# Modulation sums along rows, operand tiles placed 128 bytes in or out of step, a fifth slot in the weight ring, and the linear attention's operands written in place

## The chip, the cores and the metric

The kernel runs on one core of a Trainium2 chip. The metric is the device time of one execution in microseconds. Before the change it is 2567.68 us, the median of 3 timed runs (2567.05 to 2570.22). A profile was taken of one further execution.

## The reference

All tensors are float32. There are 256 tokens of width 2048. The first block has two layers of `x = x + concat(conv, differential attention, memory attention) @ w_out`, all fed from one product `rmsnorm(x) @ w_in`. The second block is a token mixer and a feed-forward network, both modulated by a vector that is worked out from `c`:

```
c_act = silu(c)
mod = c_act @ w_mod + b_mod                     # 2048 -> 6 * 2048
sh1, sc1, g1, sh2, sc2, g2 = split(mod, 6)
h = rms_norm(x, mix_norm_pre) * (1 + sc1) + sh1
y = token_mixer(h, ...)                         # window attention + gated linear attention
x = x + g1 * rms_norm(y, mix_norm_post)
h = rms_norm(x, ffn_norm_pre) * (1 + sc2) + sh2
y = conv_ffn(h, w_up, conv_w, conv_b, w_down)
x = x + g2 * rms_norm(y, ffn_norm_post)
```

In the gated linear attention, `q_in = q * exp(b)` and `k_st = k * exp(b_last - b)` are made for each head, besides `q * exp(b - b_mid)` and `k * exp(b_mid - b)`. In the FFN, `u = h @ w_up` goes through a causal convolution of width 3, and `(silu(gate) * val) @ w_down` gives y, with 5632 gate and 5632 value columns.

## The kernel before

**Precision.** Every large product is made of three. An operand is split into a high part (rounded to the type fp32r) and the low part that is left over, and hi x hi, hi x lo and lo x hi are added up in PSUM; "a triple" is these three matmuls. `gemm_as` (lines 354 to 356) holds x stationary and streams the weight, 512 columns wide. `gemm_ws` (lines 406 to 408) holds the weight stationary and streams x, 256 tokens wide. `gemm_wsu` (lines 428 to 430) is like `gemm_ws` with 258 columns. The split tiles of x are pairs: C and D (hi and lo), or A and B.

**The weight ring.** All weights come as pieces of 512 KB, 128 partitions x 1024 elements, in one list. `load` (line 222) issues a piece's DMA on SP's queue into one of four slots (`RB`, tile `raw`). `consume` splits a weight piece: ACT copies raw to `hi`, DVE writes `lo` = raw - hi, each with four buffers (`HB`). Right behind that in the program stands the load of the piece four places further on, which has to wait until the slot's readers are done. 847 pieces are weights of products, and 192 are of `w_mod`.

**The order.** The program is written out in its final order; nothing reorders it on an engine. Beside the pieces run small generators (attention, norms, convolution, evacuations), which `tick` moves on after every item. `await_tasks(name)` runs ticks until a generator has set the flag of that name. `spread_mod` puts the 192 modulation pieces between the weight pieces: 64 in the layers, 96 in the mixer, 32 in the FFN, and in stretches marked heavy at 0.45 of the density.

**The modulation.** A piece of `w_mod` holds 2 x 128 rows (k, on partitions) of 512 columns. DVE multiplies each row block with its 128 values of silu(c) (`ca`, one per partition) and adds it to `macc` [128 x 512]: two instructions a piece, and eight pieces to a block of 512 columns. Then `mod_done` adds up over the partitions: DVE makes two transposes within 32 x 32 blocks and two reductions into `mred`, and after four such blocks PE multiplies `mred` with a matrix of ones (into a bank `pb`), and four DVE additions write the result plus `b_mod` to `modT`, which holds one column of 128 values per block.

**Where the tiles lie.** A, B, C, D and the buffers of hi and lo are of 16 KB per partition or smaller multiples of 256 bytes. C and D (`hT`, the normalised x of the mixer and the FFN) follow each other 16,384 bytes apart. A is 128 bytes longer, since in other places it holds the 258-wide tiles, so B begins 16,512 bytes behind A. `pair_AB` gives A and a view of B that is shifted by 32 elements (128 bytes), so that it begins a multiple of 256 bytes behind A; the mixer uses it for the linear attention's output `obT`. The FFN's `gv`, the operand of `w_down`, are A and B as they are. Here "in step" is a pair whose distance is a multiple of 256 bytes, and "out of step" one that is 128 bytes off.

**The products.** The layers' `w_in` streams A and B through `gemm_ws`, out of step. The mixer's three merging products and its `w_out` (1400 to 1720 us) use `gemm_as`. The FFN's `w_up` has 176 pieces, 16 of them through `gemm_wsu` and 160 through `gemm_ws` with C and D, 8 triples each; its `w_down` has 88 pieces of 4 triples through `gemm_as` and its variant for halves (lines 379 to 381), with A and B.

Except for matmuls, most instructions are recorded by one helper, so they have line 133 in the profile (145 after the change, as 12 lines are added above it). Its tiles are told by name: `tm`, `t1k`, `e2k` are scratch, `ml` and `mh` the merged operand.

Of the kernel before, what the change touches and what calls it, by code (L numbers as in the profile page):

```python
# [6 lines left out]
F32 = mybir.dt.float32  # L7
F32R = mybir.dt.float32r
# [3 lines left out]
ALU = mybir.AluOpType  # L12
AX = mybir.AxisListType

P = 128
D = 2048
# [5 lines left out]
C_ID, C_ONE, C_INV, C_SWA, C_SCAN, C_GLA, C_SUM, C_DIST, C_END = 0, 128, 256, 288, 672, 928, 1056, 1184, 1696  # L22
# [4 lines left out]
R_BMOD, R_CW2, R_CB2 = 256, 352, 616  # L27
# [33 lines left out]
    return [512] * (n // 512)  # L61


def row_tiles(n):

    return 16 if n == 16 else 1024 // n


def lay_pieces(np, name, w):

    layers, rows, n = w.shape
    out, c0 = np.empty((layers, rows * n), w.dtype), 0
    for width in cuts(name, n):
        src = w[:, :, c0:c0 + width].reshape(layers, -1, row_tiles(width), P, width).transpose(0, 1, 3, 2, 4)
        out[:, rows * c0:rows * (c0 + width)].reshape(src.shape)[:] = src
        c0 += width
    assert c0 == n
    return out
# [75 lines left out]


class Kernel:
    RB = 4
    HB = 4
    NBG = 3
    CAP = 4.5  # L160
# [302 lines left out]
    def setup(self, ctx):  # L463
        nc, tc, a = self.nc, self.tc, self.a
        pool = lambda name, **k: ctx.enter_context(tc.tile_pool(name=name, bufs=1, **k))
        self.cp = pool("consts")
        self.wp = pool("weights")
        self.ap = pool("acts")
        dp = pool("dram", space=bass.MemoryType.DRAM)
        self.scr = {n: dp.tile(s, F32, tag=n, name=n) for n, s in (  # L470
            ("x1", [2 * P, D]), ("x2", [2 * P, D]), ("x3", [2 * P, D]), ("gp1", [D]), ("gp2", [D]))}
        self.psA = ctx.enter_context(tc.tile_pool(name="psA", bufs=2, space=bass.MemoryType.PSUM))
        psB = pool("psB", space=bass.MemoryType.PSUM)
        self.ps = Slots(psB, "pb", 4, 512)
        self.tm = Slots(self.ap, "tm", 4, 1024)
        self.sm = Slots(self.cp, "sm", 14, 16)
        self.t1 = Slots(self.ap, "t1k", 2, 256)

        cst = self.cp.tile([P, C_DIST], F32, tag="cst", name="cst")
        self.cst = cst  # L480
        self.ident = cst[:, C_ID:C_ID + P]
        self.ones = cst[:, C_ONE:C_ONE + P]
        self.junk = self.cp.tile([P, 512], mybir.dt.bfloat16, tag="junk", name="junk")
        self.mhalf = self.cp.tile([P, 16], F32, tag="mhalf", name="mhalf")
        self.cols = self.cp.tile([P, 704], F32, tag="cols", name="cols")
        self.modT = self.cp.tile([P, 96], F32, tag="modT", name="modT")
        raw = self.st["xraw"] = self.ap.tile([P, 16, 256], F32, tag="X16", name="xraw")
        for k in range(2):
            self.x_load(k, 1, nc.act_dma)
        nc.vector.memset(self.mhalf, -0.5)  # L490
        self.sg = self.sm_tile("sg", [P, 6])
        self.ca = self.sm_tile("ca", [P, 16])
        nc.scalar.activation(out=self.ca, in_=self.mhalf, func=AF.Identity)
        self.warm_up()
# [15 lines left out]
    def params(self):  # L510
        nc, a = self.nc, self.a
        nc.sync.dma_start(out=self.cols[:, 64:], in_=a["cols"][:, 64:])
        pos = self.sm_tile("pos_i", [P, 2], I32)
        nc.sync.dma_start(out=pos, in_=a["pos_cols"])
        yield
        for _ in range(6):
            yield
        nc.vector.tensor_copy(self.col(R_POS, 2), pos)


        th = self.sm.get()
        nc.scalar.activation(out=th, in_=self.col(R_C, 16), func=AF.Tanh, scale=0.5)
        nc.vector.scalar_tensor_tensor(out=self.ca, in0=th, scalar=1.0, in1=self.col(R_C, 16), op0=ALU.add, op1=ALU.mult)
        nc.vector.tensor_scalar(out=self.ca, in0=self.ca, scalar1=0.5, scalar2=None, op0=ALU.mult)
        self.sm.put(th)
        yield


        for l in range(2):
            for j, (r, s) in enumerate(((R_DQ, 0.125), (R_MQ, P ** -0.5), (R_HG, 1.0 - self.lam_init(l)))):  # L530
                nc.vector.tensor_scalar(out=self.sg[:, 3 * l + j:3 * l + j + 1], in0=self.col(r + l), scalar1=s,
                                        scalar2=None, op0=ALU.mult)

        yield
        self.st["params"] = True

    def params_attn(self):
        nc, a = self.nc, self.a
# [56 lines left out]

    def plan_mod(self):

        nc = self.nc
        self.mod_queue = deque()
        w = self.weight("w_mod_2")  # L600
        for j in range(24):
            box = {}
            for k0 in range(0, 16, 2):
                def fn(raw, j=j, k0=k0, box=box):
                    if k0 == 0:
                        if j > 1:
                            self.await_tasks(f"red{j - 2}", bg=False)
                        box["acc"] = self.cp.tile([P, 512], F32, tag="macc", name=self.nm("macc"), bufs=2)
                    acc = box["acc"]
                    for kk in range(2):  # L610
                        s = self.ca[:, k0 + kk:k0 + kk + 1]
                        if k0 + kk == 0:
                            nc.vector.tensor_scalar(out=acc, in0=raw[:, kk], scalar1=s, scalar2=None, op0=ALU.mult)
                        else:
                            nc.vector.scalar_tensor_tensor(out=acc, in0=raw[:, kk], scalar=s, in1=acc,
                                                           op0=ALU.mult, op1=ALU.add)
                    if k0 == 14:
                        self.evac.append(self.mod_done(j, acc))
                src = w.piece(k0, 2, j * 512, 512)
                self.mod_queue.append(Item("mod", fn, src, 2, 512))  # L620

    def mod_done(self, j, acc):

        nc = self.nc
        yield
        if j % 4 == 0:
            self.mred = self.cp.tile([P, 64], F32, tag="mred", name=self.nm("mred"), bufs=2)
        red = self.mred
        while not self.t1.ok():
            yield  # L630
        for h in range(2):
            tr = self.t1.get()
            nc.vector.transpose(tr, acc[:, 256 * h:256 * h + 256])
            b = 16 * (j % 4) + 8 * h
            nc.vector.tensor_reduce(out=red[:, b:b + 8], in_=tr.rearrange("p (b i) -> p b i", i=32), axis=AX.X, op=ALU.add)
            self.t1.put(tr)
        self.st[f"red{j}"] = True
        if j % 4 < 3:
            return
        yield  # L640
        yield
        pt = self.bank()
        nc.side.matmul(pt[:, 0:64], self.cst[:, C_SUM:C_SUM + P], red, start=True, stop=True)
        for q in range(4):
            b = slice(32 * q, 32 * q + 32)
            nc.vector.tensor_tensor(out=self.modT[b, 4 * j - 12:4 * j + 4],
                                    in0=pt[b, 0:64].rearrange("p (c q) -> p q c", q=4)[:, q],
                                    in1=self.cols[b, R_BMOD + 4 * j - 12:R_BMOD + 4 * j + 4], op=ALU.add)
        self.ps.put(pt)
        for i in range(4):  # L650
            self.st[f"mod{j - i}"] = True

    def mod_row(self, gcol, postcol, dst):

# [237 lines left out]
    def layer(self, l, last):  # L892
        nc, st, a = self.nc, self.st, self.a
# [136 lines left out]
        def out_begin():  # L1030
# [8 lines left out]
            if last:  # L1039
                self.await_tasks(*[f"mod{j}" for j in range(8)])  # L1040
                self.shifted("G1", R_MIXPRE, 16, 0)
                st["raw"] = [self.lp.tile([P, 4, 256], F32, tag=t, name=self.nm("raw")) for t in ("dv", "dg", "mkT", "mg")]
            else:
                st["xT2"] = [self.ap.tile([P, 16, 256], F32R, tag=t, name=self.nm(t)) for t in ("A", "B")]
# [305 lines left out]
    def shift_norm(self):  # L1350
# [15 lines left out]
        self.t1.put(dg)  # L1366
        self.ps.put(pt)
        st["r_ready"] = True
        hi, lo = [self.ap.tile([P, 16, 256], F32R, tag=t, name=self.nm(t)) for t in ("C", "D")]
        st["hT"] = (hi, lo)  # L1370
        us = [raws[k // 4][:, k % 4:k % 4 + 2] for k in range(0, 16, 2)]
        for i in range(9):
# [238 lines left out]
    def gla_pair(self, c):  # L1611
# [5 lines left out]
        for hh in range(2):  # L1617
# [1 line left out]
            q, k = qb[:, 2 * hh:2 * hh + 2], kb[:, 2 * hh:2 * hh + 2]  # L1619
            Bh = st["b"][:, 2 * h:2 * h + 2]  # L1620
            b8 = v8(Bh)
            Q, K, QI, KS, K2, QD = V(0), V(1), V(2), V(3), V(4, (2, P)), V(5, (2, 64))
            while not self.e2.ok(2):
                yield
            d, e = self.e2.get([P, 2, 256]), self.e2.get([P, 2, 256])
# [331 lines left out]
    def open_f(self):  # L1957
# [4 lines left out]
        self.st["raw"] = [self.fp.tile([P, 4, 256], F32, tag=f"raw{n}", name=self.nm("raw")) for n in range(4)]  # L1962
        self.st["u"] = 0
        self.st["h_ready"] = self.st["r_ready"] = self.st["u_done"] = False

    def add_x(self, n, tb):

# [30 lines left out]
    def ffn(self):  # L1998
# [153 lines left out]
        for part in range(3):  # L2152
            chunks = range(4 * part, min(4 * part + 4, 11))

            def alloc():
                st["gv"] = [self.ap.tile([P, 16, 256], F32R, tag=t, name=self.nm(t)) for t in ("A", "B")]

            self.do(alloc)
            for i in chunks:
# [102 lines left out]
```

## Time and profile before

| | us |
|---|---|
| median of 3 timed runs | 2567.68 (2567.05 to 2570.22) |
| the profiled execution | 2563.99 |
| its span, first to last instruction | 2562.2 |
| DVE: the 847 splits (lo) | 1026.8 |
| DVE: the modulation's STT of 512 elements, 360 at 749 ns | 269.7 |
| DVE: its transposes and reductions, 48 each | 20.9 + 20.2 |
| PE: idle in the whole span | 35.4 |
| DMA: loaded and stored | 576.77 MB, mean 225 GB/s |

Times are of the profiled execution unless the table says otherwise. PE is TensorE, PEld its weight loads (they overlap the matmuls), DVE VectorE, ACT ScalarE, POOL GpSimd, SP SyncE, whose queue issues the loads. A row of a group gives line, engine, operation, output<-input, shapes, the number of them, busy time, the mean of one in ns, and behind the last bar the idle time ahead of them and what ended it. Matmuls are pipelined, so their durations overlap: the pace is the distance between starts. "STT" is SCALAR_TENSOR_TENSOR.

### The profile page before, as it was taken

How to read it: one execution, taken by the hardware profiler on the slowest of the kernel's cores; microseconds unless marked ns; L12 is line 12 of the kernel's file. 1: busy time of each engine (PE TensorE's matmuls, PEld its weight loads, DVE VectorE, ACT ScalarE, POOL GpSimd, SP SyncE). 2: the span in 40 equal slices, each digit the busy share in tenths (PEclk: the TensorE clock that was granted, in tenths of full speed). 3: DMA queues.
4: the chain of work that ended last, by engine and by line, in shares of the span. 5: the costliest groups of instructions: out<-in, count | busy, mean ns of one | idle time of the engine just before them, and what ended most of it. 6: DMA issues, size and time to landing. Idle time of an engine off the chain costs nothing.

```text
span 2562.2 us, 38632 instructions
## 1 busy us (share of the span) xinstructions
PE 2526.8 (99%) x15079; PEld 2227.7 (87%) x15079; DVE 1823.1 (71%) x2469; ACT 1266.9 (49%) x1826; POOL 52.0 (2%) x43
## 2 busy tenths in 40 slices
PE   9999999999999999999999999999999999999998
PEld 7889998788899989878988778777999899988996
DVE  6768767786786756777777777775777667765665
ACT  6645544564554455355454334344744444543443
POOL 1000000010010000000000000000000000000000
PEclk9999999999999999999999999999999999999999
DMA  8775568887656576755558888886566766676655
GB/s 311 225 255 181 179 197 271 299 272 256 220 179 190 180 249 187 224 173 190 193 182 267 285 290 286 280 289 210 164 215 231 230 215 214 223 236 197 198 188 174
DMA packets 168903, 576.77 MB, mean 225 GB/s; under 512 B 18272, under 2 KB 24576, under 8 KB 168720
## 3 DMA queue, kind: packets, MB, share of 16 engines
q1 hardware_dynamic: 168432, 574.04, 69.0%
q8 instruction: 118, 1.93, 0.3%
q14 instruction: 65, 0.53, 0.1%
q10 hardware_dynamic: 288, 0.26, 0.0%
HBM read 565.83 MB, written 8.40 MB: 224 GB/s over the span
## 4 chain that ended last, share of the span: by engine, by line
PE 77%; DMA 9%; DVE 8%; ACT 3%; issue 2%; POOL 0%; ACTq 0%; DVEq 0%; POOLq 0%
PE acc L355 13%; PE acc L356 13%; PE acc L354 13%; PE acc L406 10%; PE acc L407 10%; PE acc L408 10%; PE pb L133 5%; DMA raw<-w_in 4%; DVE lo L133 4%; ACT hi L133 2%; DMA raw<-w_out 2%; DMA raw<-w_branch_gla 1%; DVE macc L133 1%; DMA raw<-w_branch_attn 1%; DVE tm L133 1%
## 5 line engine op out<-in xcount | busy, mean ns | idle before, releaser
L133 DVE TENSOR_TENSOR lo<-raw,hi 128x1024 fp32r<-128x1024 f32 (+1 forms) x847 | 1026.8, 1220 | 515.7 <-ACT hi L133 511.2
L133 ACT CAST hi<-raw 128x1024 fp32r<-128x1024 f32 (+1 forms) x847 | 881.7, 1048 | 867.6 <-PE acc L356 281.4
L408 PE MATMUL acc<-C,lo 128*128 128x256 f32 (+1 forms) x1424 | 403.0, 283 | 0.8 <-DVE lo L133 0.8
L406 PE MATMUL acc<-C,hi 128*128 128x256 f32 (+1 forms) x1424 | 403.7, 284 | 0.0
L407 PE MATMUL acc<-D,hi 128*128 128x256 f32 (+1 forms) x1424 | 402.9, 283 | 0.0
L354 PE MATMUL acc<-hi,C 128*128 128x512 f32 x992 | 393.1, 396 | 0.0
L355 PE MATMUL acc<-lo,C 128*128 128x512 f32 x992 | 387.4, 390 | 4.0 <-DVE lo L133 3.9
L356 PE MATMUL acc<-hi,D 128*128 128x512 f32 x992 | 387.0, 390 | 0.0
L355 PE MATMUL acc<-lo,A 128*128 128x512 f32 x904 | 357.7, 396 | 1.2 <-DVE lo L133 1.1
L356 PE MATMUL acc<-hi,B 128*128 128x512 f32 x904 | 357.9, 396 | 0.0
L354 PE MATMUL acc<-hi,A 128*128 128x512 f32 x904 | 354.2, 392 | 0.7 <-ACT hi L133 0.7
L133 DVE SCALAR_TENSOR_TENSOR macc<-raw,ca,macc 128x512 f32<-128x512 f32 x360 | 269.7, 749 | 9.9 <-DMA raw<-w_mod 2.9
L406 PEld LDWEIGHTS acc<-C,hi 128*128 128x128 f32 (+1 forms) x1424 | 271.7, 191 | 1.5 <-issue 0.7
L408 PEld LDWEIGHTS acc<-C,lo 128*128 128x128 f32 (+1 forms) x1424 | 271.7, 191 | 1.4 <-DVE lo L133 1.0
L407 PEld LDWEIGHTS acc<-D,hi 128*128 128x128 f32 (+1 forms) x1424 | 271.8, 191 | 0.6
L406 PE MATMUL acc<-A,hi 128*128 128x256 f32 x896 | 256.3, 286 | 0.0
L407 PE MATMUL acc<-B,hi 128*128 128x256 f32 x896 | 252.0, 281 | 0.0
L408 PE MATMUL acc<-A,lo 128*128 128x256 f32 x896 | 251.2, 280 | 0.3 <-DVE lo L133 0.2
L355 PEld LDWEIGHTS acc<-lo,C 128*128 128x128 f32 x992 | 186.4, 188 | 45.5 <-DVE lo L133 7.9
L354 PEld LDWEIGHTS acc<-hi,C 128*128 128x128 f32 x992 | 186.3, 188 | 40.5 <-issue 3.4
L356 PEld LDWEIGHTS acc<-hi,D 128*128 128x128 f32 x992 | 186.2, 188 | 39.3
L354 PEld LDWEIGHTS acc<-hi,A 128*128 128x128 f32 x904 | 172.7, 191 | 40.9 <-ACT hi L133 1.6
(269 smaller groups left out, 2989.5 us busy)
## 6 DMA issues: line engine op xcount, KB each, us to landing
raw<-w_in SPq DMA_DIRECT2D x406, 512.0 KB, 4.4
raw<-w_mod SPq DMA_DIRECT2D x192, 512.0 KB, 4.6
raw<-w_up SPq DMA_DIRECT2D x176, 512.0 KB, 4.2
raw<-w_out SPq DMA_DIRECT2D x96, 512.0 KB, 4.5
raw<-w_down SPq DMA_DIRECT2D x88, 512.0 KB, 4.3
raw<-w_mem_kv SPq DMA_DIRECT2D x32, 512.0 KB, 4.4
raw<-w_branch_gla SPq DMA_DIRECT2D x32, 512.0 KB, 4.7
tm<-x SPq DMA_DIRECT2D x20, 512.0 KB, 6.2
```

The source lines that it names most:

```text
L133: return f(*args, **kw)
L354: nc.tensor.matmul(o, xh[:, kt, t], hi, start=s, stop=False)
L355: nc.tensor.matmul(o, xh[:, kt, t], lo, start=False, stop=False)
L356: nc.tensor.matmul(o, xl[:, kt, t], hi, start=False, stop=e)
L406: nc.tensor.matmul(o, hi[:, c], xh, start=s and j % 2 == 0, stop=False, skip_group_check=True)
L407: nc.tensor.matmul(o, hi[:, c], xl, start=False, stop=False, skip_group_check=True)
L408: nc.tensor.matmul(o, lo[:, c], xh, start=False, stop=e, skip_group_check=True)
```

## The change

1. **Modulation.** The host lays `w_mod` out by output columns: a piece is 128 columns (on partitions) by 1024 of the 2048 k. One DVE instruction per piece (`tensor_tensor_reduce`, written in place over raw) multiplies it with `crow`, a tile that holds half of silu(c) on every partition, and sums along the row into one column of `mpart` (first half) or `modT` (second half, begun from `mpart`). The pieces' order is `MOD_GROUPS`: in each of three groups of blocks all first halves, then all second ones. So `crow` is filled six times, once by `c_row` (PE transposes `ca`, DVE copies it out, a DMA writes it to DRAM, another one reads it back to all partitions) and five times by `crow_load`, two ticks after the last sum on the old half. A sum waits for its half. `mod_done`, with its transposes, reductions, matmuls and additions, is gone; one addition of `b_mod` for four blocks takes its place.
2. **Ring.** `RB` is 5 instead of 4.
3. **Linear attention.** QI and KS are written over q and k, and K2 and QD take the tiles V2 and V3. V4 and V5 are gone.
4. **Tiles.** In the FFN, `hT`'s low tile D begins 32 elements (128 bytes) later (`skew`), and `gv` uses `pair_AB`. The mixer's `hT` keeps a skew of 0.

The core of the diff:

```diff
+MOD_GROUPS = ((0, 8), (8, 20), (20, 24))
+def mod_order():
+    return [(h, b) for j0, j1 in MOD_GROUPS for h in range(2) for b in range(4 * j0, 4 * j1)]
...
+    if name == "w_mod_2":
+        half = [w[:, 1024 * h:1024 * h + 1024, P * b:P * b + P].transpose(0, 2, 1) for h, b in mod_order()]
+        return np.stack(half, 1).reshape(layers, rows * n)
...
-    RB = 4
+    RB = 5
...
+        self.mpart = self.cp.tile([P, 96], F32, tag="mpart", name="mpart")
+        self.crow = self.cp.tile([P, 1024], F32, tag="crow", name="crow")
...
-        for j in range(24):
-            box = {}
-            for k0 in range(0, 16, 2):
-                def fn(raw, j=j, k0=k0, box=box):
...
-                            nc.vector.scalar_tensor_tensor(out=acc, in0=raw[:, kk], scalar=s, in1=acc,
-                                                           op0=ALU.mult, op1=ALU.add)
-                    if k0 == 14:
-                        self.evac.append(self.mod_done(j, acc))
+        order = mod_order()
+        for i, (h, b) in enumerate(order):
+            def fn(raw, i=i, h=h, b=b):
+                self.await_tasks(f"crow{self.mod_half[i]}", bg=False)
+                d = raw.rearrange("p k n -> p (k n)")
+                out = self.mpart[:, b:b + 1] if h == 0 else self.modT[:, b:b + 1]
+                nc.vector.tensor_tensor_reduce(out=d, in0=d, in1=self.crow, scale=1.0,
+                                               scalar=0.0 if h == 0 else self.mpart[:, b:b + 1], op0=ALU.mult, op1=ALU.add,
+                                               accum_out=out)
+                if h and b % 4 == 3:
+                    j = b // 4
+                    nc.vector.tensor_tensor(out=self.modT[:, b - 3:b + 1], in0=self.modT[:, b - 3:b + 1],
+                                            in1=self.col(R_BMOD + b - 3, 4), op=ALU.add)
+                    self.st[f"mod{j}"] = True
+                if i + 1 < len(order) and self.mod_half[i + 1] != self.mod_half[i]:
+                    self.evac.append(self.crow_load(self.mod_half[i + 1]))
...
+    def crow_load(self, m):
+        for _ in range(2 if m else 0):
+            yield
+        h = m % 2
+        self.nc.sync.dma_start(out=self.crow, in_=self.scr["crow"][1024 * h:1024 * h + 1024].partition_broadcast(P))
+        self.st[f"crow{m}"] = True
...
-        hi, lo = [self.ap.tile([P, 16, 256], F32R, tag=t, name=self.nm(t)) for t in ("C", "D")]
+        hi = self.ap.tile([P, 16, 256], F32R, tag="C", name=self.nm("C"))
+        lo = self.ap.tile([P, 16 * 256 + 64], F32R, tag="D", name=self.nm("D"))
+        s = st["skew"]
+        lo = lo[:, s:s + 4096].rearrange("p (k t) -> p k t", t=256)
...
-            Q, K, QI, KS, K2, QD = V(0), V(1), V(2), V(3), V(4, (2, P)), V(5, (2, 64))
+            Q, K, QI, KS, K2, QD = V(0), V(1), q, k, V(2, (2, P)), V(3, (2, 64))
...
+        self.st["skew"] = 32
...
-                st["gv"] = [self.ap.tile([P, 16, 256], F32R, tag=t, name=self.nm(t)) for t in ("A", "B")]
+                st["gv"] = self.pair_AB()
```

DVE, at the end of the mixer's modulation, in `w_out` of the mixer: what stood there before (`macc` is the running sum, `mred` its reduction, `pb` a PSUM bank that PE has filled).

```order
L133 SCALAR_TENSOR_TENSOR macc_15328<-raw_15538,ca,macc_15328 128x512 x2
L133 TENSOR_TENSOR lo_15604<-raw_15556,hi_15603 128x1024
L133 TENSOR_TENSOR lo_15628<-raw_15578,hi_15627 128x1024
L133 SCALAR_TENSOR_TENSOR ml<-pb_213_15621,mh 128x512
L133 STREAM_TRANSPOSE t1k_78_15648<-macc_15328 128x256
L133 TENSOR_REDUCE mred_14730<-t1k_78_15648 128x8
L133 STREAM_TRANSPOSE t1k_79_15651<-macc_15328 128x256
L133 TENSOR_REDUCE mred_14730<-t1k_79_15651 128x8
L133 TENSOR_TENSOR lo_15655<-raw_15584,hi_15654 128x1024
L133 TENSOR_TENSOR modT<-pb_214_15672,cols 32x16 x4
```

And the same place on DVE after the change (an ISA row of 128x1024 is the new product with its sum, and the ISA row of 128x1 behind it reads the sum out).

```order
L145 ISA raw_15192,modT<-raw_15192,crow,mpart 128x1024
L145 ISA modT 128x1
L145 TENSOR_TENSOR lo_15285<-raw_15218,hi_15284 128x1024
L145 SCALAR_TENSOR_TENSOR ml<-pb_209_15275,mh 128x512
L145 ISA raw_15237,modT<-raw_15237,crow,mpart 128x1024
L145 ISA modT 128x1
L145 TENSOR_TENSOR modT<-modT,cols 128x4
L145 TENSOR_TENSOR lo_15308<-raw_15243,hi_15307 128x1024
```

The four rows of transposes and reductions between two splits are gone, and so are PE's matmul over `mred` and the four additions that waited for it; a piece has one long and one short row instead of two rows of 512.

SP's queue after the change, where the mixer goes from the window attention's merge (`w_branch_attn`) on to the gate columns of `w_in`, and `crow` is filled for the second half of the second group:

```order
L234 DMA raw_13497<-w_mod 128x1024
L234 DMA raw_13521<-w_branch_attn 128x1024
L234 DMA raw_13537<-w_mod 128x1024
L234 DMA raw_13543<-w_branch_attn 128x1024
L234 DMA raw_13567<-w_branch_attn 128x1024
L234 DMA raw_13583<-w_mod 128x1024
L234 DMA raw_13589<-w_in 128x1024
L646 DMA crow<-crow 128x1024
L234 DMA raw_13605<-w_in 128x1024
```

DVE at that place: the first row is the last sum on the old half, and the fourth, over raw_13537, is the first on the new one.

```order
L145 ISA raw_13497,mpart<-raw_13497,crow 128x1024
L145 ISA mpart 128x1
L145 TENSOR_TENSOR lo_13586<-raw_13521,hi_13585 128x1024
L145 ISA raw_13537,modT<-raw_13537,crow,mpart 128x1024
L145 ISA modT 128x1
L145 TENSOR_TENSOR lo_13608<-raw_13543,hi_13607 128x1024
L145 TENSOR_TENSOR lo_13628<-raw_13567,hi_13627 128x1024
```

Before, nothing of this was on SP's or DVE's queue; the load of `crow` now stands five loads behind that of raw_13537, and one split stands between the last reader of the old `crow` and the first of the new one.

More of the change, by code (lines that the diff above doesn't have):

```diff
@@ L470, in setup @@
         self.scr = {n: dp.tile(s, F32, tag=n, name=n) for n, s in (
-            ("x1", [2 * P, D]), ("x2", [2 * P, D]), ("x3", [2 * P, D]), ("gp1", [D]), ("gp2", [D]))}
+            ("x1", [2 * P, D]), ("x2", [2 * P, D]), ("x3", [2 * P, D]), ("gp1", [D]), ("gp2", [D]), ("crow", [D]))}
         self.psA = ctx.enter_context(tc.tile_pool(name="psA", bufs=2, space=bass.MemoryType.PSUM))
@@ L535, in params @@
         self.st["params"] = True
+        for _ in range(6):
+            yield
+        yield from self.c_row()
     def params_attn(self):
@@ L599, in plan_mod @@
         self.mod_queue = deque()
-        w = self.weight("w_mod_2")
-        for j in range(24):
-            box = {}
-            for k0 in range(0, 16, 2):
-                def fn(raw, j=j, k0=k0, box=box):
[L605 to L614, printed above, removed]
-                            nc.vector.scalar_tensor_tensor(out=acc, in0=raw[:, kk], scalar=s, in1=acc,
-                                                           op0=ALU.mult, op1=ALU.add)
-                    if k0 == 14:
-                        self.evac.append(self.mod_done(j, acc))
-                src = w.piece(k0, 2, j * 512, 512)
-                self.mod_queue.append(Item("mod", fn, src, 2, 512))
@@ L622, in mod_done @@
-    def mod_done(self, j, acc):
-        nc = self.nc
-        yield
[L626 to L639, printed above, removed]
+        order = mod_order()
@@ new lines, in plan_mod @@
+        for i, (h, b) in enumerate(order):
[13 more added lines that the diff above has]
+                    self.evac.append(self.crow_load(self.mod_half[i + 1]))
+            src = self.a["w_mod_2"][0][i * P * 1024:(i + 1) * P * 1024].rearrange("(p k n) -> p k n", p=P, k=2)
+            self.mod_queue.append(Item("mod", fn, src, 2, 512))
@@ new lines, in plan_mod, with c_row @@
+        self.mod_half, m = [], -1
+        for i, (h, b) in enumerate(order):
+            m += i == 0 or h != order[i - 1][0]
+            self.mod_half.append(m)
+    def crow_load(self, m):
+        for _ in range(2 if m else 0):
+            yield
+        h = m % 2
+        self.nc.sync.dma_start(out=self.crow, in_=self.scr["crow"][1024 * h:1024 * h + 1024].partition_broadcast(P))
+        self.st[f"crow{m}"] = True
+    def c_row(self):
+        nc = self.nc
+        pt = self.bank()
+        self.transpose(pt[:16, :P], self.ca)
+        row = self.t1.get([P, 256])
+        nc.vector.tensor_copy(row[:16, :P], pt[:16, :P])
+        self.ps.put(pt)
+        yield
+        nc.sync.dma_start(out=self.scr["crow"].rearrange("(k p) -> k p", p=P), in_=row[:16, :P])
+        self.t1.put(row)
@@ L640, in mod_done @@
         yield
         yield
[L642 to L648, printed above, removed]
@@ L649, in mod_done @@
-        self.ps.put(pt)
-        for i in range(4):
-            self.st[f"mod{j - i}"] = True
+        yield from self.crow_load(0)
     def mod_row(self, gcol, postcol, dst):
@@ L1041, in out_begin @@
                 self.shifted("G1", R_MIXPRE, 16, 0)
+                st["skew"] = 0
                 st["raw"] = [self.lp.tile([P, 4, 256], F32, tag=t, name=self.nm("raw")) for t in ("dv", "dg", "mkT", "mg")]
```

## The prediction

> **What bounds the kernel now.** The head of the profile's page and its chain come first.
>
> ```profile
> span 2562.2 us, 38632 instructions
> PE 2526.8 (99%) x15079; PEld 2227.7 (87%) x15079; DVE 1823.1 (71%) x2469; ACT 1266.9 (49%) x1826; POOL 52.0 (2%) x43
> ...
> PE 77%; DMA 9%; DVE 8%; ACT 3%; issue 2%; POOL 0%; ACTq 0%; DVEq 0%; POOLq 0%
> ```
>
> PE is busy for all but 35 us, so the time falls in two ways only: its matmuls follow each other faster, or it waits less. The chain leaves PE for DMA, DVE and ACT during a fifth of the span. To see where, I read the busy time by stage (PE, PEld, DVE, ACT and POOL, then the granted clock, the DMA share and GB/s).
>
> ```profile
> core 0: us, PE busy (x) PEld busy (x) DVE busy (x) ACT busy (x) POOL busy (x), PEclk, DMA share, GB/s
> 500.00:520.00 20.00, 19.19 (x84) 15.44 (x83) 15.39 (x28) 13.29 (x20) 2.20 (x2) 1.00 0.95 335
> 1400.00:1720.00 320.00, 307.01 (x1336) 246.30 (x1335) 251.38 (x304) 124.93 (x125) 0.00 (x0) 0.99 0.86 288
> 200.00:300.00 100.00, 100.00 (x791) 95.38 (x788) 81.31 (x140) 58.89 (x132) 7.20 (x7) 1.00 0.55 174
> ```
>
> The stretch 1400 to 1720 is the merge of the mixer and its last product. 13.0 of PE's 35 idle us lie there (320.00 less 307.01); 200 to 300 has none. The waits of that stretch, first PE's, then its weight loads', then ACT's (us, times, longest):
>
> ```profile
> PE acc L355 <- DVE lo L133: 5.0, 11, 0.8
> PE pb L133 <- DVE tm L133: 4.2, 3, 2.1
> PE pb L133 <- DVE mred L133: 3.5, 2, 3.3
> ```
> ```profile
> PEld acc L355 <- DVE lo L133: 12.4, 20, 1.1
> PEld pb L133 <- DVE tm L133: 5.7, 4, 2.6
> PEld pb L133 <- DVE mred L133: 4.4, 2, 3.8
> ```
> ```profile
> ACT hi L133 <- DMA raw<-w_in: 83.3, 47, 4.1
> ACT hi L133 <- DMA raw<-w_branch_gla: 44.7, 27, 3.6
> ...
> ACT hi L133 <- PE acc L356: 3.1, 2, 2.7
> ```
>
> PE waits for the split of a piece (lo), and for two small DVE results. DVE is not full (251 of 320). ACT, a step earlier, waits 128 us for landings of two weights and hardly for PE: the pieces come late, not the consumers. The chain from 1410 (start, length) shows why.
>
> ```profile
> 1409.99 5.50 DMA raw<-w_in
> ...
> 1415.60 1.07 ACT hi L133
> ...
> 1416.69 1.24 DVE lo L133
> 1417.94 4.17 DMA raw<-w_branch_gla
> ...
> 1424.55 5.98 DMA raw<-w_branch_gla
> ...
> 1431.72 1.23 DVE lo L133
> ```
>
> Each load starts when the split before it has freed a slot. A slot's turns take 7.95, 6.61 and 8.40 us (1409.99, 1417.94, 1424.55, 1432.95), 7.65 on average: with four slots, one piece every 1.91 us. The stage consumes 110 weight pieces and 62 of modulation (rows below), one every 1.86 us. So this stretch is bound by the **ring of four slots**, and the rest by PE's own pace.
>
> **The change, part by part.**
>
> *Tiles in step.* Four stretches of uninterrupted triples in PE's timeline, first and last row of each (start, length), 11 triples in the first two and 6 in the others:
>
> ```profile
> 854.91 0.28 PE L406 MATMUL acc<-A,hi 128*128 128x256 f32 x1
> ...
> 858.76 0.28 PE L406 MATMUL acc<-A,hi 128*128 128x256 f32 x1
> ```
> ```profile
> 2110.03 0.28 PE L406 MATMUL acc<-C,hi 128*128 128x256 f32 x1
> ...
> 2113.99 0.28 PE L406 MATMUL acc<-C,hi 128*128 128x256 f32 x1
> ```
> ```profile
> 1422.60 0.39 PE L354 MATMUL acc<-hi,A 128*128 128x512 f32 x1
> ...
> 1426.68 0.39 PE L354 MATMUL acc<-hi,A 128*128 128x512 f32 x1
> ```
> ```profile
> 2282.26 0.39 PE L354 MATMUL acc<-hi,A 128*128 128x512 f32 x1
> ...
> 2286.42 0.39 PE L354 MATMUL acc<-hi,A 128*128 128x512 f32 x1
> ```
>
> With the weight stationary, the triple takes 350 ns from A and B (3.85 us over 11) and 360 from C and D (3.96 over 11). With x stationary, it takes 680 ns on the mixer's A and B (4.08 over 6) and 693 on the FFN's (4.16 over 6), with the same names and shapes. What differs is where the low tile begins: 16,384 bytes after the high one (C and D) or 128 more (A and B, whose shifted view in pair_AB brings it back to a multiple of 256). So stationary weights want the pair 128 bytes out of step, and stationary x wants it in step; the change gives the FFN both. The price of the wrong phase is 10 and 13.3 ns a triple. w_up has 176 pieces, 16 of them go through the 258-wide product, and the other 160 have 8 triples: 1280 x 10 = 12.8 us, of which I take **-12**, since busier stretches may hold less. w_down has 88 pieces of 4: 352 x 13.3 = **-4.7**. Both are PE's pace and lie on the path; bounds 0 and -17.5 together. All tiles also begin 96 bytes further on modulo 256; no row here tells what that does, and I take nothing for it.
>
> [...]
>
> *The modulation sums.* DVE's groups in the ring's stretch, and one of the whole run:
>
> ```profile
> L133 DVE TENSOR_TENSOR lo<-raw,hi 128x1024 fp32r<-128x1024 f32 x110 | 134.2, 1224 | 63.3 <-ACT hi L133 62.6
> L133 DVE SCALAR_TENSOR_TENSOR macc<-raw,ca,macc 128x512 f32<-128x512 f32 x117 | 87.7, 749 | 3.4 <-DMA raw<-w_mod 1.1
> ...
> L133 DVE STREAM_TRANSPOSE t1k<-macc 128x256 f32<-128x256 f32 x16 | 7.0, 436 | 0.0
> L133 DVE TENSOR_REDUCE mred<-t1k 128x8 f32<-128x256 f32 x16 | 6.7, 421 | 0.6
> ...
> L133 DVE TENSOR_SCALAR macc<-raw,ca 128x512 f32<-128x512 f32 x7 | 3.4, 480 | 0.0
> L133 DVE TENSOR_TENSOR modT<-pb,cols 32x16 f32<-32x16 f32 x8 | 1.3, 168 | 0.1
> ```
> ```profile
> L133 DVE TENSOR_TENSOR_SCAN b<-cst,gk 128x256 f32<-128x256 f32 x8 | 5.1, 679 | 0.1
> ...
> L133 DVE TENSOR_TENSOR t1k<-acc,cos 128x256 f32<-128x256 f32 x8 | 3.4, 423 | 1.0 <-PE acc L356 0.8
> ```
>
> 117 and 7 halves make 62 pieces. The old sums cost 87.7 + 7.0 + 6.7 + 3.4 + 1.3 = 106.1 us here. The new one is one product with a sum over 1024 elements, which the trace lacks. The nearest row is lo, two f32 sources of the same shape: 1.22 us. From below the 1024 elements could go at TENSOR_SCALAR's 480 ns for 512, 0.96 us; from above stands the scan, whose 256 elements take 256 ns more than a plain product, 1 ns an element, so 1.22 + 1.02 = 2.24 us. I take 1.22, plus 0.17 for the second row that reads the sum out (the 32x16 row). Then 62 x 1.39 + about 8 x 0.17 for the bias adds is 87.6: DVE is 18.5 us less busy there, unseen except through the waits below.
>
> [...]
>
> *The fifth slot.* The same turn of 7.65 us spread over five slots gives a piece every 1.53 us. PE needs 110 pieces x 12 matmuls x 0.227 us (the 680 ns above, by three) = 300 us, 1.74 a piece over 172, so PE becomes the bound again, if the DMA can go at 0.524 MB / 1.74 us = 301 GB/s. It went at 335 for 20 us. What goes of the waits: those for mred altogether, as PE's sums over it no longer exist (3.5 in PE's list, 4.4 in the loads': 3.9); those for lo (5.0 and 12.4, mean 8.7) by four fifths, 7.0; those for tm (4.2 and 5.7), which stand behind splits and modulation sums on DVE, by two fifths, 2.0. Together **-13**; the bounds are 0 and the whole 22.5 of the loads' list. Late next is DVE's own queue.
>
> *The sums' matmuls.* All of PE's, and PE's waits for lo in the whole run:
>
> ```profile
> L133 PE MATMUL pb<-mred,cst x12: 217/273/423, 483.9 to 2324.6; 128*128 128x64 f32 x12
> ```
> ```profile
> PE acc L355 <- DVE lo L133: 6.9, 14, 0.9
> ```
>
> Twelve records at 0.27 us, overlapping by half: **-1.5** (0 to -3.3). Of the lo waits 1.9 lie outside the stage; with a deeper ring most go: **-1.5** (0 to -1.9).
>
> *The row of c.* Five reloads of the tile that every new sum reads. The next sum, and all of DVE behind it, waits for the landing, and so do the splits that PE needs. Each is 512 KB, and starts two ticks after the last sum on the old half. Three of the five have a long time before the next modulation piece. In the order, the mixer's reload stands on SP five loads behind the piece that its user multiplies, and on DVE one split lies between the last sum on the old half and that user: about 1.2 us of cover against 4.2 to 6.0 for a landing (the chain above), so DVE stops for some 4 us. PE then lives on splits made ahead, up to three, each good for 2.7 us (12 x 0.227). I take **+3** (0 to +8), and **+1** (0 to +4) for the one at the layers' boundary. The first c row is made beside the start's other side work, at nothing.
>
> *The rest.* The linear attention's operands written into q and k change no instruction; they could only add a wait where the old tile is still read. For its bound I take one lo row, 1.22 us, in each of the four heads, 4.9 us; PE has other items there and hardly idles outside the ring's stretch, so nothing.
>
> Sum: -12 - 4.7 - 13 - 1.5 - 1.5 + 3 + 1 = -28.7 on the profiled execution's 2564.0 us (its span and 1.8 us around it): 2535.3. That execution lies 3.7 below the median of the runs shown, 2567.7, so the forecast is **2539**.
>
> **The rivals.**
>
> *R1, the tile shifts give nothing*, or the 96 bytes take as much elsewhere. For: no row here has stationary weights on C and D out of step, and the fifth slot moves every tile. Against: the 10 and 13.3 ns come from like shapes at one clock. 2539 + 16.7 = 2556.
>
> *R2, the product with a sum runs at half speed.* At the scan's price DVE has 251.4 - 106.1 + 62 x (2.24 + 0.17) + 1.4 = 296 us of work in the ring's stretch of 320. The densest 100 us that the trace shows are at 0.81; at 0.9 the stretch takes 329, at 0.81 366, in the middle 347, 27 more instead of 13 less. Elsewhere 130 pieces cost 0.7 us more each, mostly hidden: +5. So 2539 + 40 + 5 = 2584, slower than before. It decides from where the stretch takes 320 us at a density of 0.85, 272 us of work: a sum of (272 - 146.7) / 62 = 2.02 us with its read.
>
> *R3, the fifth slot only lengthens the landings*, or the reloads eat it. For: at 0.86 the DMA queues are nearly full, and a transfer that shares them with four others ends later; then the pace stays at 1.86 us. Against: 335 GB/s at 500. Only mred's 3.9 goes, and 2539 + 9 + 4 = 2552.
>
> **How the numbers follow.** Forecast 0.66, with its own range of 2527 to 2553 (the whole of the ring's waits gone and no reload waited for, 12 less; half of the ring's gain and dear reloads, 14 more). R1 0.13, R3 0.13, R2 0.08. The range of 2526 to 2561 holds the forecast and R1 and R3, and leaves out R2 and sums of R1 and R3. A measurement of this kernel tells about 0.2%, 5.1 us, from no change. Faster by more: the forecast, nearly all of R1 and R3, 0.87; within it: both of them together, or a sum at about 2 us, 0.06; slower: most of R2, 0.07.
>
> **What would show it.** The FFN's triples: 350 instead of 360 and 680 instead of 693. The new sum's row: 1.2 to 1.3 us, with a second row below 0.2. Between about 1400 and 1700: no wait for mred, those for lo below 3 us on PE, ACT waiting for PE and not for landings, over 300 GB/s. In the mixer one wait of DVE for the reload, of 3 to 5 us, with PE idle for less. It is wrong if the sum takes over 2 us, if landings grow by as much as the fifth slot gains, or if triples elsewhere (the layers' 350, the mixer's 680) get longer.

## The result and the profile after

The changed kernel takes 2526.97 us (median of 4 runs, 2525.40 to 2527.49) against 2567.36 us for the kernel before in the same session (4 runs, 2564.64 to 2570.22): a ratio of 0.9842, with a 95% interval of 0.9824 to 0.9859, so 40 us or 1.6% faster. The forecast was 2539, 28 us faster. The profiled execution of after took 2527.14 us, 36.85 less than that of before.

The head of the page of after, and its chain:

```profile
span 2525.3 us, 38525 instructions
## 1 busy us (share of the span) xinstructions
PE 2503.0 (99%) x15068; PEld 2217.2 (88%) x15068; DVE 1747.5 (69%) x2374; ACT 1265.4 (50%) x1826; POOL 53.6 (2%) x43
...
PE 95%; DVE 3%; ACT 1%; issue 1%; DMA 0%; SPq 0%; POOL 0%; POOLq 0%; DVEq 0%; ACTq 0%
```

DMA, which was 9% of the chain, is gone from it, and PE went from 77% to 95%. To place the gain, each weight matmul of after was set beside the same one of before (both have 14064 of them in the same order). The difference of their start times is -3.4 us at the matmul that stood at 1400 in the kernel before, -23.9 at 1720, still -23.9 at 1772, and -37.0 at the last one. So 20.4 us come from the mixer's merge and `w_out`, 13.1 from the FFN, and 3.4 from what lies ahead.

The same stretch of work as 1400 to 1720 before now takes 299.4 us, by the starts of its first and last matmul (by stage, columns as before):

```profile
1396.80:1696.70 299.90, 298.83 (x1334) 246.93 (x1333) 225.79 (x273) 124.63 (x124) 0.00 (x0) 1.00 0.88 304
```

PE is full, at 304 GB/s where 301 were asked for. Its waits there are one row, its loads' waits one, and ACT now waits for PE and no longer chiefly for landings (PE, PEld, ACT):

```profile
PE acc L367 <- DVE lo L145: 1.1, 1, 1.1
```
```profile
PEld acc L367 <- DVE lo L145: 1.5, 1, 1.5
```
```profile
ACT hi L145 <- PE acc L368: 107.9, 71, 1.7
ACT hi L145 <- DMA raw<-w_in: 26.0, 12, 5.4
...
ACT hi L145 <- DMA raw<-w_branch_gla: 11.1, 9, 2.9
```

The new sums on DVE, by shape: the product with its sum for second halves (which begin from `mpart`), the same for first halves, and the reads of the result.

```profile
L145 DVE CUSTOM_DVE_ANT_0 raw<-raw,crow,mpart 128x1024 f32<-128x1024 f32 x96 | 122.8, 1279 | 13.0 <-issue 6.8 <-DMA crow<-crow 6.0 <-DMA raw<-w_mod 0.2
L145 DVE CUSTOM_DVE_ANT_0 raw<-raw,crow 128x1024 f32<-128x1024 f32 x96 | 116.8, 1217 | 0.0
...
L145 DVE DVE_READ_ACCUMULATOR2_ANT mpart<- 128x1 f32 x96 | 7.9, 82 | 0.0
```

1.22 to 1.28 us, and 0.08 for the read. The nearest row, lo of the same shape, has 1223 ns over its 842 pieces of 128x1024: first halves (1217) are no slower, second halves (1279) by 56 ns. So the rival R2 did not happen.

The FFN's triples, 11 with the weight stationary and 6 with x stationary, from PE's timeline of after:

```profile
1899.87 0.28 PE L418 MATMUL acc<-C,hi 128*128 128x256 f32 x1
...
1903.76 0.27 PE L418 MATMUL acc<-C,hi 128*128 128x256 f32 x1
```
```profile
2010.23 0.39 PE L366 MATMUL acc<-hi,A 128*128 128x512 f32 x1
...
2014.31 0.39 PE L366 MATMUL acc<-hi,A 128*128 128x512 f32 x1
```

353.6 ns and 680.0 ns a triple. Over the whole FFN the means are 353.3 and 680.3, where the kernel before has 360.0 and 693.5.

The reload in the merge, on DVE (the idle time ahead is in brackets) and on PE:

```profile
1460.09 1.22 DVE L145 TENSOR_TENSOR lo<-raw,hi 128x1024 fp32r<-128x1024 f32 x1
1468.07 1.29 DVE L145 CUSTOM_DVE_ANT_0 raw<-raw,crow,mpart 128x1024 f32<-128x1024 f32 x1 [6.75 <-issue]
```
```profile
1469.09 0.39 PE L366 MATMUL acc<-hi,oaT 128*128 128x512 f32 x1
1470.55 0.50 PE L367 MATMUL acc<-lo,oaT 128*128 128x512 f32 x1 [1.07 <-DVE lo L145]
```

DVE stood for 6.75 us. The row names no releaser ("issue"), but the load of `crow` was issued at 1461.7 and took 6.2 us to land, so at 1467.9, and DVE went on at 1468.07: this is the reload. PE went on with splits made ahead until one was late by 1.46 - 0.23 = 1.23 us (the distance between the two starts, less the usual one). The row's own figure is 1.07: a matmul's modelled end lies behind the start of the next one (0.39 us long, 0.227 apart), so this wait is short by 0.16 us in PE's list.

### The profile page after: what moved, and what is told of

Same layout as the page of the kernel before. It is cut to its first block, busy times and chain, and to the rows that moved or that the text cites. A ratio compares the mean times of both kernels' runs of the same rounds, so it can differ in the third digit from the quotient of the medians.

```text
span 2525.3 us, 38525 instructions
## 1 busy us (share of the span) xinstructions
PE 2503.0 (99%) x15068; PEld 2217.2 (88%) x15068; DVE 1747.5 (69%) x2374; ACT 1265.4 (50%) x1826; POOL 53.6 (2%) x43
## 4 chain that ended last, share of the span: by engine, by line
PE 95%; DVE 3%; ACT 1%; issue 1%; DMA 0%; SPq 0%; POOL 0%; POOLq 0%; DVEq 0%; ACTq 0%
PE acc L368 18%; PE acc L367 18%; PE acc L366 18%; PE acc L419 11%; PE acc L418 11%; PE acc L420 11%; PE pb L145 5%; DVE lo L145 1%; PE acc L440 1%; PE acc L441 1%; PE acc L442 1%; PE pb L393 0%; PE pb L392 0%; PE pb L391 0%; ACT hi L145 0%
## 5 line engine op out<-in xcount | busy, mean ns | idle before, releaser
L419 PEld LDWEIGHTS acc<-D,hi 128*128 128x128 f32 (+1 forms) x1424 | 266.3, 187 | 0.6
L367 PEld LDWEIGHTS acc<-lo,A 128*128 128x128 f32 x904 | 169.8, 188 | 37.4 <-DVE lo L145 1.2
```

The lines of the kernel that those rows point to most:

```text
L367: nc.tensor.matmul(o, xh[:, kt, t], lo, start=False, stop=False)
L419: nc.tensor.matmul(o, hi[:, c], xl, start=False, stop=False, skip_group_check=True)
```

## The experiments

All were timed beside the kernel before. Its median was 2565.2 us in the session of "Four slots again", "The tiles as before", "The slot alone" and "Both tiles of each pair moved", and 2564.8 in that of the other four. A ratio is to the kernel before; "slower than after" is the distance to the 2526.97 us of the result. As the kernel before differs by up to 2.6 us between the three sessions, the last two us of such a distance say little.

### Four slots again

```diff
-    RB = 5
+    RB = 4
```

> The changed kernel with four slots in the weight ring again; all else stays. Theory S (the slot): what made the stretch of the mixer's merge and w_out 20.7 us shorter is that a slot's turn of about 7.65 us is spread over five pieces instead of four. Then the stalls for lo and tm come back (some 14 us of the 18 us of stalls; those for mred stay gone): about 2540 us, ACT waiting for landings again. Theory V (DVE's load): it is the 18 us less that DVE has to do there, and the slot is hardly needed: 2527 to 2531 us, PE without stalls.

2546.4 us, ratio 0.9931 (0.9909 to 0.9953): 19 us slower than after. The slot is needed, as theory S said, and ACT waits for landings again (72.1 us for `w_in` alone). The stretch (by stage, weight loads' waits there, DVE's waits in the whole run):

```profile
1406.20:1718.40 312.20, 302.72 (x1332) 247.17 (x1332) 226.49 (x274) 123.47 (x124) 0.00 (x0) 0.99 0.86 291
```
```profile
PEld acc L367 <- DVE lo L145: 8.5, 6, 5.6
PEld pb L145 <- DVE tm L145: 2.3, 3, 1.0
```
```profile
DVE raw L145 <- DMA crow<-crow: 12.5, 2, 6.4
```

It was not as expected in its places, though. Set beside after, matmul by matmul, 6.6 us are lost between 487 and 547 and 5.8 us between 1450 and 1510, and at both places DVE waits 6 us for a reload of `crow`; one lo is 5.6 us late. With five slots the same two waits cost PE 1.2 us together. So two thirds of the 19 us lie at the new wait, laid bare by the shorter ring; the rest is put down to the ring's turn.

The two long waits of this run cost PE more than their idle time. They stand in PE's list with 3.57 and 5.22 us. Behind them 11 and 8 matmuls start 0.43 to 0.59 us apart instead of 0.227, which is 4 us more, and the granted clock (the third figure from the end) is low around both:

```profile
491.30:500.00 8.70, 5.13 (x13) 3.69 (x12) 7.04 (x8) 1.36 (x2) 0.00 (x0) 0.69 0.52 179
1478.60:1487.80 9.20, 3.98 (x11) 2.81 (x9) 4.77 (x6) 1.63 (x2) 0.00 (x0) 0.63 0.56 167
```

### The tiles as before

```diff
-        self.st["skew"] = 32
+        self.st["skew"] = 0
...
-                st["gv"] = self.pair_AB()
+                st["gv"] = [self.ap.tile([P, 16, 256], F32R, tag=t, name=self.nm(t)) for t in ("A", "B")]
```

> The changed kernel with the FFN's tiles as they were before (C and D in step, A and B out of step). Theory P (phase): the triples with the weight stationary go back from 353.4 to 360 ns (1280 x 6.6 = 8.4 us) and those with x stationary from 680 to 693.5 ns (352 x 13.5 = 4.7 us): about 2540 us. Rival (the whole layout moved by 96 bytes, and the distance in a pair does nothing): 2527 us, triples of 353 and 680 ns.

2539.4 us, ratio 0.9902 (0.9886 to 0.9918): 12.4 us slower than after. The triples (11 and 6) are back:

```profile
1900.06 0.28 PE L418 MATMUL acc<-C,hi 128*128 128x256 f32 x1
...
1904.02 0.28 PE L418 MATMUL acc<-C,hi 128*128 128x256 f32 x1
```
```profile
2009.85 0.39 PE L366 MATMUL acc<-hi,A 128*128 128x512 f32 x1
...
2014.01 0.39 PE L366 MATMUL acc<-hi,A 128*128 128x512 f32 x1
```

360 and 693 ns. The layout is as far along as in after, so the 96 bytes by which the prediction has all tiles moved (no row shows an address) do nothing here; theory P holds, and its rival falls.

### The slot alone, with the old sums and tiles

In the kernel before:

```diff
-    RB = 4
+    RB = 5
...
-            Q, K, QI, KS, K2, QD = V(0), V(1), V(2), V(3), V(4, (2, P)), V(5, (2, 64))
+            Q, K, QI, KS, K2, QD = V(0), V(1), q, k, V(2, (2, P)), V(3, (2, 64))
```

> The kernel before with five slots and the linear attention in place (which makes room for the slot), but the old modulation sums and the old tiles. Theory S: the stalls for lo and tm go (14 us), those for mred stay (4 us): about 2553 us. Theory V: the old sums keep DVE as loaded as before, so the slot gains little: 2562 to 2567 us.

2539.9 us, ratio 0.9902 (0.9886 to 0.9917): 25 us faster than before, which neither theory had. (The operands in place, whose room the slot needs, were not run by themselves.) The stretch by stage, and ACT's waits there:

```profile
1398.00:1696.50 298.50, 298.50 (x1335) 247.12 (x1335) 248.19 (x302) 124.90 (x124) 0.00 (x0) 1.00 0.89 305
```
```profile
ACT hi L133 <- PE acc L356: 124.2, 82, 1.9
ACT hi L133 <- DMA raw<-w_in: 17.0, 8, 3.3
```

PE never waits there, although DVE does all its old work (248 us). Not only the waits for lo and tm are gone but also those for mred, which the forecast had given to the new sums. The reading of this is that with a ring that runs ahead splits lie ready, and PE does not run into DVE's queue. This kernel is 21.4 us shorter in the stretch (319.8 to 298.5), no less than after (20.4).

### The whole change without the new sums

The kernel of the last experiment, with the FFN's tiles as in after; `mred` has one buffer instead of two, for room:

```diff
...
+        lo = self.ap.tile([P, 16 * 256 + 64], F32R, tag="D", name=self.nm("D"))
+        s = st["skew"]
+        lo = lo[:, s:s + 4096].rearrange("p (k t) -> p k t", t=256)
...
+        self.st["skew"] = 32
...
+                st["gv"] = self.pair_AB()
...
-            self.mred = self.cp.tile([P, 64], F32, tag="mred", name=self.nm("mred"), bufs=2)
+            self.mred = self.cp.tile([P, 64], F32, tag="mred", name=self.nm("mred"), bufs=1)
```

> The kernel before with the fifth slot, the linear attention in place and the FFN's tiles as after, that is the whole change without the new modulation sums (to make room, mred has one buffer instead of two). Theory A (the sums and the slot heal the same stalls, and the slot alone heals them all): as the changed kernel, 2525 to 2529 us. Theory B (the sums bring something of their own through 75 us less work on DVE): 5 us or more above the changed kernel, 2532 us or more.

2528.4 us, ratio 0.9852 (0.9837 to 0.9867). The interval of after, 0.9824 to 0.9859, holds this ratio, and the profiled spans are 2526.8 and 2525.3: theory A. The stretch of the ring is as in the experiment before:

```profile
1399.00:1697.50 298.50, 298.50 (x1336) 247.04 (x1335) 248.22 (x302) 124.34 (x124) 0.00 (x0) 1.00 0.89 306
```

The new sums take 72 us of DVE's work away (1819.7 us busy here, 1747.5 in after) and bring no time that can be told from none.

### Four slots and two tiles of c

```diff
-    RB = 5
+    RB = 4
...
-        self.crow = self.cp.tile([P, 1024], F32, tag="crow", name="crow")
+        self.crow = [self.cp.tile([P, 1024], F32, tag=f"crow{h}", name=f"crow{h}") for h in range(2)]
...
-                if i + 1 < len(order) and self.mod_half[i + 1] != self.mod_half[i]:
-                    self.evac.append(self.crow_load(self.mod_half[i + 1]))
...
+        for h in range(2):
+            self.nc.sync.dma_start(out=self.crow[h], in_=self.scr["crow"][1024 * h:1024 * h + 1024].partition_broadcast(P))
```

> The changed kernel with four slots, and two tiles of c, loaded once each at the start in the room of the fifth slot, so that no reload is waited for. With one tile and four slots (2546 us) the two places of a reload lost 6.6 us near 490 to 556 and 5.8 us near 1450 to 1510. Theory R (the reload, which keeps DVE waiting while a ring of four runs dry): 12 us less, 2534 us, with few stalls left in the merge. Theory S alone (the slot's turn): at most 3 us less, 2543 us or more.

2536.8 us, ratio 0.9891 (0.9874 to 0.9907): 9.6 us less than four slots with reloads, where 12 were expected (the profiled executions differ by 11.9). By matmuls set beside those of after, nothing is lost between 1450 and 1510 any more, and 1.1 of the 6.6 us between 487 and 547 are left. So theory R holds for most of it. Not few stalls are left in the merge, though: between 1371 and 1732 the distances over 330 ns still lose 8.3 us (13.5 with four slots and reloads), which no reload explains. The stretch, and its weight loads' waits:

```profile
1399.70:1706.50 306.80, 302.27 (x1332) 246.88 (x1331) 227.01 (x275) 123.58 (x124) 0.00 (x0) 0.99 0.88 295
```
```profile
PEld acc L367 <- DVE lo L145: 3.8, 6, 1.1
PEld pb L145 <- DVE tm L145: 3.0, 3, 1.1
```

This is what the new sums are worth by themselves: with four slots they bring the stretch from 320 to 307 us, 13 of the 21 that the slot brings. Against a kernel with four slots, the old sums and the FFN's new tiles (2564.8 - 12.4 = 2552, worked out and not run) they save 16 us, of which only these 13 lie in the stretch; with five slots, nothing that can be told from none. Both parts heal the same stalls.

### Both tiles of each pair moved away from the weights

In the FFN, C moves like D, and A moves 128 bytes too while B is taken as it lies. This run and the next also drop 128 columns of constants that nothing reads any more (not shown):

```diff
-        hi = self.ap.tile([P, 16, 256], F32R, tag="C", name=self.nm("C"))
+        hi = self.ap.tile([P, 16 * 256 + 64], F32R, tag="C", name=self.nm("C"))
...
+        hi = hi[:, s:s + 4096].rearrange("p (k t) -> p k t", t=256)
...
-                st["gv"] = self.pair_AB()
+                hi, lo = [self.ap.tile([P, 16 * 258], F32R, tag=t, name=self.nm(t)) for t in ("A", "B")]
+                st["gv"] = [hi[:, 32:32 + 4096].rearrange("p (k t) -> p k t", t=256),
+                            lo[:, 0:4096].rearrange("p (k t) -> p k t", t=256)]
```

> The changed kernel with both tiles of each pair of the FFN moved 128 bytes away from the weights' hi and lo: C and D both begin 32 elements later, A too, with B out of step with hi and lo by itself. Within a pair the tiles are in step. Theory D (what counts is the distance within the pair): w_up's triples return to 360 ns, w_down's stay at 680 ns: about 2535 us. Theory W (what counts is the distance between the tile of x and the tiles of the weight, which PE reads at the same time): w_up's triples stay at 353 ns or fall to 350 or below, w_down's rise to 693 ns or more: 2522 to 2532 us.

2539.2 us, ratio 0.9899 (0.9883 to 0.9914), 12.2 us slower than after. The triples of `w_up` (11 each, in its first stretch and in its second) and of `w_down` (6):

```profile
1899.99 0.28 PE L417 MATMUL acc<-C,hi 128*128 128x256 f32 x1
...
1903.91 0.28 PE L417 MATMUL acc<-C,hi 128*128 128x256 f32 x1
```
```profile
2100.16 0.28 PE L417 MATMUL acc<-C,hi 128*128 128x256 f32 x1
...
2104.12 0.28 PE L417 MATMUL acc<-C,hi 128*128 128x256 f32 x1
```
```profile
2009.95 0.39 PE L365 MATMUL acc<-hi,A 128*128 128x512 f32 x1
...
2014.13 0.40 PE L365 MATMUL acc<-hi,A 128*128 128x512 f32 x1
```

`w_up` takes 356 ns in its first stretch, between the two theories, and 360 in its second, as D has it. In the third it goes from 360 to 356 near 2378, with the same tiles. Over the FFN its mean is 358.1. `w_down` takes 697 to 700 ns (mean 698.3), worse than before, which speaks for W and against D. With x stationary, then, and in these three placements, the distance to the weight's tiles counts, not that within the pair. The means account for the time: 1280 x 4.8 + 352 x 18 ns = 12.5 us.

### The high tile moved instead of the low one

The tile of C gets the 64 elements of room that D's had, and the shift goes to C:

```diff
...
-        lo = lo[:, s:s + 4096].rearrange("p (k t) -> p k t", t=256)
+        hi = hi[:, s:s + 4096].rearrange("p (k t) -> p k t", t=256)
```

> The changed kernel with the FFN's C moved by 128 bytes instead of D; w_down's tiles as after. The distance within the pair is the same, but now the high tile, which two of three matmuls stream, is out of step with the weights, and the low one in step with them. Theory D (the distance within the pair): triples of 353 ns, 2527 us. Theory W (the distance to the weight tiles, by how many of the three matmuls stream such a tile): below 353, 350 or less, 2523 us or less. With both away the triples took 356 ns, which speaks for neither by itself.

2535.5 us, ratio 0.9883 (0.9868 to 0.9898), 8.5 us slower than after; 11 triples take 3.96 us, 360 ns each, and 359.9 is the mean over the FFN:

```profile
1899.98 0.28 PE L417 MATMUL acc<-C,hi 128*128 128x256 f32 x1
...
1903.94 0.28 PE L417 MATMUL acc<-C,hi 128*128 128x256 f32 x1
```

Both theories fall: with the same distance in the pair nothing is gained, and neither is it by moving the tile that two of three matmuls stream. Of the two, only the low one moved alone gains.

### A shift of 64 bytes

```diff
-        self.st["skew"] = 32
+        self.st["skew"] = 16
```

> The changed kernel with D moved by 64 bytes instead of 128. If any distance that is no multiple of 256 does: 353 ns a triple, 2527 us. If the gain grows with the distance: about 357 ns, 2531 us. If only 128 does: 360 ns, 2535 us.

2527.2 us, ratio 0.9850 (0.9836 to 0.9865), as after; the triples:

```profile
1899.89 0.28 PE L418 MATMUL acc<-C,hi 128*128 128x256 f32 x1
...
1903.77 0.28 PE L418 MATMUL acc<-C,hi 128*128 128x256 f32 x1
```

353 ns. Here 64 bytes do as much as 128 (353.6 in after).

## Why the prediction was right, and where its sizes were off

The direction was right, and so was the account of the ring: with four slots the pieces come late, and a fifth gives the bound back to PE. Two accounts were not: what the new sums bring by themselves, and the rule for the tiles. The measured time lies in the range, 1 us above its lower end. The forecast was 12.0 us too slow. About 3.9 of that is the step from the profiled execution to the median: 3.7 us were added for it, and after's lies 0.2 above its median. The other 8.2 are terms of the sum, and in them two misses partly cancel: outside the FFN 12.0 us were forecast and 23.9 came, in the FFN 16.7 and 13.1. That the time still fell into the range is in part luck.

- **The fifth slot, forecast -13.** The mechanism was right: ACT waits for PE, PE is the bound, and the DMA goes as fast as was asked. The size was the largest miss. The whole stretch gained 20.4 us where slot, sums' matmuls and reload were to give 10.8 (13 and half of the 1.5, less 3). The step that failed took fractions of the lists of waits ("four fifths", "two fifths"), from a mean of PE's list and the loads'. Worked out from the starts in the kernel before, 45 distances between one matmul and the next in the stretch (a little widened, 1371 to 1732) are over 330 ns; they add up to 30.1 us, and 45 x 0.227 = 10.2 of it is normal: 19.9 us lost. PE's list had 12.7 and the loads' list, named as the upper bound, 22.5. PE's list is short in two ways. 19 of the distances hold an idle time, and each costs some 0.17 us more than the list has, as at 1470.55: 3.2 us. The other 26 hold none and lose 3.7 us, as the matmul behind a late one is slow too. The longest wait, 3.33 us for mred until 1715.78, is followed by seven distances of 0.42 to 0.57 us, 1.5 us more, and the clock granted from 1712 to 1719.3 is 0.77. Nearly all of these stalls went in the new kernel, not a fraction: with the slot alone no distance over 330 ns is left, and even a stall that names DVE's sums as its releaser is gone.
- **The new sums: right price, wrong account.** 1.30 and 1.36 us a piece with its read, where 1.39 was taken; in the stretch's two windows the rows of the sums fall from 106.1 us for 62 pieces to 84.2 for 61, with 87.6 forecast. But the forecast credited them with mred's 3.9 us as something that only they could bring. The slot alone brings it too, and the run without the new sums is as fast as the whole. What they took away was not on the path any more.
- **Tiles, forecast -16.7, measured 12.4 by undoing them.** `w_down` gave its 4.7: 680 ns, as forecast. For `w_up`, 350 ns came from one stretch of the layers (850 to 860), most of which run at 353 too; the FFN of after settles at 353.3, so that 1280 x 6.7 = 8.6 came instead of 12. A mean of several stretches would have been the better row. The rule behind the forecast, that stationary weights want the pair out of step and stationary x wants it in step, does not hold. With the high tile moved the pair is just as far out of step, and `w_up` stays at 360; with both tiles moved away from the weights the pair of `w_down` is in step, and it takes 697 to 700. The term came out because the change uses just the two placements whose rows the prediction had.
- **The reloads, forecast +4.** 1.2 us. DVE stood longer than the 3 to 5 us forecast (6.75), but PE had splits in store and lost little of it. With a ring of four slots the same waits took about 10 us (four slots with reloads against four without). This was the right worry for the old ring and the wrong one for the new.
- **Waits outside the stretch and the sums' matmuls, forecast -3.** 3.4 us were gained ahead of 1400; the run with the slot alone gains 2.4 between 400 and 550, without touching the sums, and after gains 2.5 there. The matmuls over mred take 0.8 us of starts between 1371 and 1732.
- **The rivals.** R1 falls with the triples of after and the run that undid the tiles. R3 falls with the loads' pace: the landing of `w_branch_gla` went only from 4.7 to 5.0 us (median), and the rate rose from 288 to 304 GB/s. R2 falls with the rows of the new product: 1217 and 1279 ns, against 1223 for lo, a plain difference of the same shape, and against the 2.24 us that R2 took from the scan.

What stays open is why the tiles' distance matters. The runs give a table, not a cause. With the weight stationary, ns a triple for (high tile, low tile) in or out of step with the weight's tiles: in, in 360; in, out 353, but 350 in the first stretch of the FFN in both runs with four slots; out, out 356 or 360 by stretch; out, in 360. With x stationary: in, in 680; in, out 693; out, out 697 to 700. No theory that was tried gives them all, and as the pace changes in one run with the same tiles (from 360 to 356 near 2378), being in or out of step is not the whole of it.

## What to carry to other kernels

When one engine waits for pieces that come through a ring, count what a slot's whole turn takes, divide by the slots, and compare it with the consumer's pace; if it is slower, as here (7.65 us over four slots is 1.91, against PE's 1.74), try one more slot besides less work on the engine that is named as the releaser: in the stretch the slot brought 21 us and the new sums 13, and both together 20. Size such a stall by the distances between the starts of the consumer's instructions, not by the idle times in its list of waits: here the matmuls behind a long wait were slow too (0.42 to 0.57 us apart instead of 0.227 behind the 3.33 us). And a new wait is to be priced with the store of finished work that the new kernel keeps, since two waits of some 6 us on DVE cost PE 1.2 us together with five slots and some 10 with four.

## What was not expected of the hardware

- Moving operand tiles by 128 bytes changed the pace of matmuls with the same shapes by 2 to 3% (360 to 353 ns a triple, 680 to 700 ns), each product in its own way, and for `w_up` a shift of 64 bytes was enough (353 ns). The places do not fix it: with the same tiles one run goes from 360 to 356 ns near 2378.
- In the kernel before and in that with four slots, the three longest waits of PE (3.33, 3.57 and 5.22 us) are each followed by 7 to 11 matmuls at about half pace (0.43 us instead of 0.227), with granted clocks of 0.77, 0.69 and 0.63 around them. The length of a wait does not decide it alone: at the FFN's start one of 2.00 us is followed by 14 matmuls of 258 columns some 0.215 us apart instead of 0.12 in the kernel before (0.66 from 1801 to 1806), and behind one of 2.06 us in the run with the slot alone the clock is full (1.00 from 1778 to 1783).
- The DVE product with a running sum over 1024 f32 elements cost what a plain difference of two such tiles cost (1217 against 1223 ns); starting the sum from a column instead of a constant added 62 ns (1279), and the read of the result 82 ns.
